# MLP weight sums moved from the up projection into the input projection; norms cut into three steps; output weights loaded one block ahead

## The chip, the cores and the metric

The kernel runs on one core of a Trainium2 chip. The metric is the device time of one execution in microseconds (us). Three executions of the kernel before took 2307.93, 2308.28 and 2311.22 us; the median is 2308.28 us.

## The reference

One layer of a streaming encoder, in float32, for 2048 prompt frames and 64 frames of a running stream (2112 tokens in all), model width 1024, MLP width 4096:

```
a = rmsnorm(h, norm1)
qa, ka, va, qr, kr, vr, gr = split(a @ w_in)          # width 2816: attention and retention heads
attn_o = windowed attention of qa, ka, va, with sinks
ret_o  = chunked retention of qr, kr, vr with decay; normed, times silu(gr)
h = h + concat(attn_o, ret_o) @ w_out
h = h + square(relu(rmsnorm(h, norm2) @ w_up)) @ w_down
y = rmsnorm(h, norm_f)
```

Outputs are y for both sets of frames, the newest 128 keys and values and the retention states.

## The kernel before, in words

Every float32 operand of a product is split into a high part h, written by ScalarE in the format fp32r, and a low part l = x - h, written by VectorE (`split`, L619: its lines are L620 and L621); each product is then three matmuls, hh, hl and lh. The kernel has four stages, one after the other.

**Input projection** (`group`, L516; main loop L570 to L587). Two phases `ph` of half the heads each; in each, 17 tiles `t` of 128 tokens (the last, `t = S = 16`, has 64); for each tile three groups `ci` of 384, 512 and 512 columns, 24 matmuls of 8 contraction blocks each (L529, L530, L532). Between the matmuls of a group, `run_ready` (L501) puts the attention and retention steps of earlier tiles (`att_b` to `att_e`, `ret_b` to `ret_e`). It is a planner with a clock of its own: `COST` (L478) is what a step takes of TensorE, `LAT` (L477) is how long after one step the next may be placed, doubled for the tiles in `slow` (L544). The pass runs under `manual_schedule` for TensorE and SyncE (L553): these two take their instructions in program order. VectorE, ScalarE and GpSimd take theirs in an order that the framework derives from a timing model when the kernel is built; the order is fixed then, and each engine runs it in order. VectorE does the rotations (L196 to L198), row maxima (L286), normalized weights (L301) and low parts here; GpSimd adds rotated parts (`zr` and `qk`, L199) and makes the low part of x (`xl`, L154). SyncE issues the loads: x of a tile (L142, one buffer `xr`), its rotation table (L160, two buffers `rt`). Weight loads go through the pool `wraw` (L74: four buffers of 4 KB a partition, tag `raw`): twelve loads at the start, twelve around the change of phase.

**Output projection** (`out_part`, L671). The 2112 tokens are three parts `p` of 704. For each of 8 output blocks `d` the weights of the block are loaded and split where they are used (L675 to L681, slots `wo`), the residual is loaded (`xres`, L683), 48 matmuls run (L690 to L692), the sum is stored to the scratch tensor `hscr` (L694), and ScalarE and GpSimd add up its squares (L696, L698). `load_mix` (L660) loads and splits the 8 mixed head blocks of a part. All of part 0 and part 1 is loaded before the first matmul (L747, L748), part 2 in a hook. `hooks` are steps put behind block `d`: the norm of the part before (`norm_part`, L704, through `norm_rs`, L623: a cast and a subtraction on VectorE, two matmuls with ones, then a scale, Sqrt on ScalarE, a reciprocal and four more steps on VectorE; twice per part, 352 columns each), and `a_sums` (L713: normed activations and their four right-hand sums, stored to `ascr`).

**Up projection** (`up_pair`, L798). Both MLP products are computed as 7 products of half-size blocks in place of 8 (the order is `ORDER`, L34). The right-hand sums come from `a_sums`. The left-hand (weight) sums are made by `left_sums` (L650): S5 = L21+L22 (L652, VectorE), S7 = L11-L21 (L653, GpSimd), S6 = S5-L11 (L654), S3 = L12-S6 (L655, both VectorE). A pass over the weights is 16 pairs `j` of 7 products of 12 matmuls, and there are three passes `p`. In pass 0, `up_weights` (L777) loads the two weight blocks of a pair, makes the sums, uses them and stores them to `uscr` (L785, L786). In passes 1 and 2 it loads the seven weights (L793), and behind each odd pair `down_sums` (L764) loads blocks of `wdn`, sums them and stores the sums to `sscr` (L774, L775). `norm_part(2)` stands behind pair 1 of pass 0 (L845); `a_operand` (L728) loads and splits the activations of the next pass behind the products of pair 15. The relu and square (L831, L832) and `right_sums` (L642) make the operands of the down projection, stored to `vscr` (L834, L835). From the output projection on, no engine is under `manual_schedule`.

**Down projection** (L948 to L1008). 84 steps of 48 matmuls (L970 to L972); it reads `wdn` or `sscr` (`left`, L863) and `vscr`, and ends with the last norm (`final_norm`, L896).

SBUF is close to full in both halves of the program. When the input projection ends (`p1.close()`, L592), the new pools lie where its pools lay, and the first writer of a new tile waits for the last reader of what lay there before (`reuse_waits="tile"`).

Of the kernel before, what the change touches and what calls it, by code (L numbers as in the profile page):

```python
# [11 lines left out]
F32 = mybir.dt.float32  # L12
# [19 lines left out]
NP = 3  # L32
# [7 lines left out]
def body(ctx, tc, xt, xtok, w1, wout, wup, wdn, gains, sinks, ck, cv, sret, rot, rdec, qdec, dmask,  # L40
# [528 lines left out]

    for i, (ph, t, ci) in enumerate(groups):  # L570
# [11 lines left out]
        group(ph, t, ci, n_)  # L582
        if (ph, ci) == (0, 2) and i == last_use[0, 2]:
            load_tables(1)
        if ph == 0 and i == last_use[0, ci]:
            ws[1, ci] = load_w(1, ci, raws)
            raws = None  # L587
    while queue:
        run_ready(1e9)
# [12 lines left out]
    wp = upper.enter_context(pool(name="wp", bufs=9, side="right"))  # L602
# [20 lines left out]
    def norm_rs(dst, acc, tmp):  # L623

        n = acc.shape[-1]
        pn_ = psum("pn_")
        ah, al = tmp("nah", F32R)[:, :n], tmp("nal", F32R)[:, :n]
        nc.vector.tensor_copy(ah, acc)
        sub(al, acc, ah.bitcast(F32))
        nc.tensor.matmul(pn_[:, :n], ones, ah, start=True, stop=False)  # L630
        nc.tensor.matmul(pn_[:, :n], ones, al, start=False, stop=True)
        m, y = tmp("nm", F32)[:, :n], tmp("ny", F32)[:, :n]
        nc.vector.tensor_scalar(m, pn_[:, :n], 1.0 / D, EPS, op0=ALU.mult, op1=ALU.add)
        nc.scalar.activation(y, m, AF.Sqrt)
        nc.vector.reciprocal(y, y)

        nc.vector.tensor_mul(m, m, y)
        nc.vector.tensor_mul(m, m, y)
        nc.vector.tensor_scalar(m, m, -0.5, 1.5, op0=ALU.mult, op1=ALU.add)
        nc.vector.tensor_mul(dst, y, m)  # L640
# [9 lines left out]
    def left_sums(sA, sB, L11, L12, L21, L22):  # L650

        add(sA[:, 0], L21, L22)  # L652
        nc.gpsimd.tensor_sub(sB[:, 0], L11, L21)  # L653
        sub(sA[:, 1], sA[:, 0], L11)  # L654
        sub(sB[:, 1], L12, sA[:, 1])  # L655

# [3 lines left out]
    def load_mix(p):  # L660
        n0 = p * PN
        out = []
        for f in range(8):
            raw = rawslot("mraw")[:, :PN]
            nc.sync.dma_start(raw, mscr[f, :, n0:n0 + PN])
            t = qp.tile([128, 2, PN], F32R, name="mhl", tag="q")
            split(t[:, 0], t[:, 1], raw)
            out.append(t)
        return out

    def out_part(p, mix, hooks):  # L671
        n0 = p * PN
        acc = None
        for d in range(NK):
            raw = rawslot("woraw")  # L675
            nc.sync.dma_start(raw, wout[d])
            w = []
            for i in range(2):
                s = wslot("wo")
                split(s[:, 0], s[:, 1], raw[:, i * 512:i * 512 + 512])  # L680
                w.append(s)  # L681
# [22 lines left out]
    def norm_part(p, acc):  # L704
        for b in range(2):
            tr, t = arslot("nr", F32R), arslot("nt")

            def tmp(name, dt):
                return (tr if dt == F32R else t)[:, int(name in ("nal", "ny"))]
            n = p * PN + b * NB  # L710
            norm_rs(rs2[:, n:n + NB], acc[:, b * NB:b * NB + NB], tmp)
# [23 lines left out]
    A, accs, mixes = {}, {}, {}  # L735
# [4 lines left out]
    def put(d, k, f, *a):  # L740
        d[k] = f(*a)

    with pool(name="op", bufs=1, side="right") as op:
        def opslot(name):
            return op.tile([128, 4, NB], F32, name=name, tag="as", bufs=2)
# [4 lines left out]
        accs[1] = out_part(1, mixes[1], {  # L750
            1: [lambda: norm_part(0, accs[0])],
            2: [later(a_sums, 0, 0, opslot), lambda: put(mixes, 2, load_mix, 2)],
            3: [later(a_sums, 0, 1, opslot)], 4: [later(a_sums, 0, 2, opslot)], 5: [later(a_sums, 0, 3, opslot)]})
        accs[2] = out_part(2, mixes[2], {
            1: [lambda: norm_part(1, accs[1]), lambda: put(A, (0, ORDER[0]), a_operand, 0, ORDER[0])],
            2: [lambda: put(A, (0, ORDER[1]), a_operand, 0, ORDER[1]), later(a_sums, 1, 0, opslot)],
            3: [lambda: put(A, (0, ORDER[2]), a_operand, 0, ORDER[2]), later(a_sums, 1, 1, opslot)],
            4: [lambda: put(A, (0, ORDER[3]), a_operand, 0, ORDER[3]), later(a_sums, 1, 2, opslot)],
            5: [later(a_sums, 1, 3, opslot)]})
        for i in ORDER[4:]:  # L760
            A[0, i] = a_operand(0, i)


    def down_sums(u):  # L764
        d, fq = u // 4, u % 4
        c = slice(fq * 512, fq * 512 + 512)
        rw = []
        for e in (d, d + 4):
            r = rawslot("dnraw").rearrange("p (a n) -> p a n", a=2)
            nc.sync.dma_start(r, wdn[e].rearrange("p (a f) n -> p a (f n)", a=2)[:, :, c])  # L770
            rw.append(r)
# [65 lines left out]
    with pool(name="up", bufs=1, side="right") as up:  # L837
        for p in range(NP):
# [114 lines left out]
    for n, (p, i, d) in enumerate(steps):  # L953
# [48 lines left out]
        for f in pending.pop(n, ()):  # L1002
            f()
# [97 lines left out]
```

## Time and profile before

| | |
|---|---|
| median of three executions | 2308.28 us |
| the profiled execution | 2315.14 us, its span 2313.3 us |
| TensorE busy | 2225.7 us (96%), mean granted clock 0.984 |
| VectorE busy | 1533.3 us (66%) |
| ScalarE busy | 1112.4 us (48%) |
| GpSimd busy | 474.2 us (20%) |
| DMA | 486.55 MB, mean 210 GB/s |

In the profile PE is TensorE's matmul, PEld its weight load, DVE VectorE, ACT ScalarE, POOL GpSimd, SP SyncE (SPq: its DMA issues). PEclk is the TensorE clock that the throttle granted, 1.00 being full speed. The view by stages gives for each stretch of the span the busy time and, in brackets, the instructions of each engine, then PEclk, the DMA share and the GB/s. The view of waits says which engine's line stood still for which other's, in us in total, how often, and the longest. The view of one line gives least, median and greatest duration in ns. The view in order of time gives start, duration, and in square brackets how long the engine was idle before and for whom it waited.

### The profile page before, as it was taken

What the parts mean: (1) busy time and instruction counts of PE and PEld (TensorE: products, weight loads), DVE (VectorE), ACT (ScalarE), POOL (GpSimd) and SP (SyncE); (2) the same over time, 40 slices, a digit from 0 to 9 for tenths busy, and PEclk for the clock granted to TensorE, in tenths of its full rate; (3) what the DMA queues carried; (4) which work ended last, traced back from release to release, by engine and by line L of the source; (5) the groups of instructions that cost most, each with busy time, mean ns of one, the idle gap of its engine ahead of it and who ended that gap; (6) DMA issues with size and microseconds to landing.
All of it is one profiled execution on the core that took longest, in us unless ns stands there. A gap on an engine that the chain in (4) does not pass through costs nothing.

```text
span 2313.3 us, 35596 instructions
## 1 busy us (share of the span) xinstructions
PE 2225.7 (96%) x13256; PEld 2117.4 (92%) x13256; DVE 1533.3 (66%) x2577; ACT 1112.4 (48%) x1985; POOL 474.2 (20%) x550
## 2 busy tenths in 40 slices
PE   7999999999997999699999999999999999999998
PEld 5888888888885999699999899999899999999998
DVE  5555556555556378887787768777766876687665
ACT  5444445443445243355555546655544544444452
POOL 5444343333332112110101000000000200020012
PEclk9999999999997999799999999999999999999999
DMA  6222233211115578866689999999986777677662
GB/s 191 79 69 69 76 95 118 61 43 52 48 33 191 177 269 290 287 233 233 232 291 355 344 321 335 335 318 303 354 286 235 253 275 259 223 270 283 237 212 78
DMA packets 242734, 486.55 MB, mean 210 GB/s; under 512 B 20560, under 2 KB 126224, under 8 KB 242560
## 3 DMA queue, kind: packets, MB, share of 16 engines
q1 hardware_dynamic: 238592, 474.40, 60.5%
q0 software_dynamic: 3968, 9.87, 1.4%
q8 instruction: 104, 1.70, 0.3%
q14 instruction: 70, 0.57, 0.1%
HBM read 348.28 MB, written 135.99 MB: 209 GB/s over the span
## 4 chain that ended last, share of the span: by engine, by line
PE 40%; DMA 9%; DVE 7%; issue 2%; ACT 1%; SPq 0%; DVEq 0%; POOL 0%; ACTq 0%
PE y L971 9%; PE y L972 9%; PE y L970 9%; DMA up<-in_wup 3%; DVE wu L621 2%; DMA upr<-uscr 2%; PE b L810 2%; PE b L811 2%; PE b L812 2%; PE a L812 1%; PE a L810 1%; PE a L811 1%; PE c L810 1%; PE c L811 1%; DMA sscr<-sd 1%
## 5 line engine op out<-in xcount | busy, mean ns | idle before, releaser
L971 PE MATMUL y<-vl,wd 128*128 128x352 f32 x1344 | 437.2, 325 | 0.0
L972 PE MATMUL y<-vh,wd 128*128 128x352 f32 x1344 | 435.0, 324 | 2.1 <-DVE wd L621 2.1
L970 PE MATMUL y<-vh,wd 128*128 128x352 f32 x1344 | 432.5, 322 | 0.3 <-ACT wd L620 0.3
L529 PE MATMUL z<-w,xh 128*128 128x512 f32 (+1 forms) x816 | 325.2, 398 | 7.1 <-ACT w L86 7.1
L530 PE MATMUL z<-w,xh 128*128 128x512 f32 (+1 forms) x816 | 309.2, 379 | 1.3 <-DVE w L87 1.3
L620 ACT ACTIVATE wd<-dr 128x1024 fp32r<-128x1024 f32 x168 | 177.3, 1057 | 254.9 <-PE y L972 176.3
L532 PE MATMUL z<-w,xl 128*128 128x512 f32 (+1 forms) x768 | 288.3, 375 | 0.5 <-POOL xl L154 0.3
L621 DVE TENSOR_TENSOR wd<-dr,wd 128x1024 fp32r<-128x1024 f32 x168 | 208.5, 1244 | 105.0 <-ACT wd L620 102.4
L972 PEld LDWEIGHTS y<-vh,wd 128*128 128x128 f32 x1344 | 252.3, 188 | 2.4 <-DVE wd L621 2.4
L970 PEld LDWEIGHTS y<-vh,wd 128*128 128x128 f32 x1344 | 253.8, 189 | 0.6 <-ACT wd L620 0.6
L971 PEld LDWEIGHTS y<-vl,wd 128*128 128x128 f32 x1344 | 251.9, 187 | 0.0
L810 PE MATMUL b<-ah,wu 128*128 128x352 f32 x576 | 187.4, 327 | 11.8 <-DVE u L821 9.4
L921 POOL TENSOR_TENSOR acc<-acc,sq 128x352 f32<-128x352 f32 x41 | 68.7, 1677 | 596.0 <-ACT sq L917 596.0
L812 PE MATMUL b<-ah,wu 128*128 128x352 f32 x576 | 186.4, 324 | 1.9 <-DVE wu L621 1.9
L811 PE MATMUL b<-al,wu 128*128 128x352 f32 x576 | 186.9, 324 | 0.0
L529 PEld LDWEIGHTS z<-w,xh 128*128 128x128 f32 x816 | 155.4, 190 | 26.0 <-ACT w L86 7.9
L620 ACT ACTIVATE wu<-upr 128x512 fp32r<-128x512 f32 x224 | 134.9, 626 | 89.8 <-DMA upr<-in_wup 50.7
L530 PEld LDWEIGHTS z<-w,xh 128*128 128x128 f32 x816 | 155.4, 190 | 22.9 <-DVE w L87 5.2
L621 DVE TENSOR_TENSOR wu<-upr,wu 128x512 fp32r<-128x512 f32 x224 | 149.7, 690 | 36.5 <-ACT wu L620 35.8
L532 PEld LDWEIGHTS z<-w,xl 128*128 128x128 f32 x768 | 144.2, 188 | 24.1 <-POOL xl L154 0.7
L621 DVE TENSOR_TENSOR vl<-rv,vh 128x1408 fp32r<-128x1408 f32 x84 | 137.2, 1638 | 37.9 <-ACT vh L620 36.4
L810 PE MATMUL a<-ah,wu 128*128 128x352 f32 x384 | 127.0, 331 | 15.2 <-ACT pc L815 8.0
(291 smaller groups left out, 4995.8 us busy)
## 6 DMA issues: line engine op xcount, KB each, us to landing
rv<-vscr SPq DMA_DIRECT2D x84, 704.0 KB, 5.5
vscr<-C SPq DMA_DIRECT2D x48, 1056.0 KB, 7.7
dr<-sscr SPq DMA_DIRECT2D x96, 512.0 KB, 4.3
dr<-in_wdn SPq DMA_DIRECT2D x72, 512.0 KB, 4.7
upr<-uscr SPq DMA_DIRECT2D x128, 256.0 KB, 6.5
upr<-in_wup SPq DMA_DIRECT2D x96, 256.0 KB, 6.4
up<-in_wup SPq DMA_DIRECT2D x32, 512.0 KB, 5.9
uscr<-su SPq DMA_DIRECT2D x32, 512.0 KB, 2.9
```

Source lines behind the costliest of these rows:

```text
L529: nc.tensor.matmul(z[:, :n], xh[:, k], wh, start=k == 0, stop=False)
L530: nc.tensor.matmul(z[:, :n], xh[:, k], wl, start=False, stop=k == NK - 1 and xl is None)
L532: nc.tensor.matmul(z[:, :n], xl[:, k], wh, start=False, stop=k == NK - 1)
L620: nc.scalar.activation(h, x, AF.Copy)
L621: sub(l, x, h.bitcast(F32))
L810: nc.tensor.matmul(o, wh, ah[:, k], start=k == 0 and i in (1, 6, 5), stop=False, skip_group_check=True)
L811: nc.tensor.matmul(o, wh, al[:, k], start=False, stop=False, skip_group_check=True)
L812: nc.tensor.matmul(o, wl, ah[:, k], start=False, stop=k == 3 and i in (2, 4, 3), skip_group_check=True)
L921: nc.gpsimd.tensor_add(self.acc, self.acc, sq)
L970: nc.tensor.matmul(o, wh, vh, start=f == 0, stop=False)
L971: nc.tensor.matmul(o, wh, vl, start=False, stop=False)
L972: nc.tensor.matmul(o, wl, vh, start=False, stop=f == 15)
```

## The change

- **Weight sums.** The sums of the up weights (32 units: block pair `j`, half `h`) and of the down weights (32 units: block `d`, one eighth of the columns) leave the up projection and are made during the input projection. A unit is 256 columns: two loads of 256 KB, four VectorE operations on 128x256, one store of 512 KB. Behind group i stand, in this order, the store of the unit that was loaded two groups earlier, the sums of the unit loaded one group earlier, and the loads of a new unit. The first unit is loaded behind group (phase 0, tile 2, 0); there are none in the groups about the change of phase nor in the first two tiles of phase 1. Loaded and summed tiles both come from `wraw`. All four sums are VectorE's; S7 was GpSimd's.
- **Up projection.** Pass 0 now reads its seven weights as the other two passes do. `down_sums` is gone. The small tiles `pc`, `u2`, `u3` are allocated together at the start of a pair.
- **Norms.** `norm_rs` becomes a class with three steps: `split`, `sums` (the matmuls with ones) and `power`. In the output projection and the first pairs of the up projection the steps of a part's norm stand behind three successive blocks or pairs, for all 704 columns at once; in the down projection behind three successive steps.
- **Output weights.** Those of block d+1 are loaded and split ahead of the matmuls of block d; those of block 0 ahead of everything else. `load_mix` loads one of 8 blocks per call; part 1's are loaded in hooks of part 0, part 2's in hooks of part 1.
- **Memory.** The pool `wp` of split weights has 8 buffers in place of 9.

```diff
+    def sum_load(u):
+        w, j, h = u // 32, u % 32 // 2, u % 2
+        r = wraw.tile([128, 4, 256], F32, name="sr", tag="raw")
+        if w == 0:
+            c = slice(h * 256, h * 256 + 256)
+            src = [wup[e].rearrange("p (a c) -> p a c", a=2)[:, :, c] for e in (j, j + 16)]
+            dst = uscr[:, j, :, c]
+        else:
...
+        for k in range(2):
+            nc.sync.dma_start(r[:, 2 * k:2 * k + 2], src[k])
+        return r, dst
+    def sum_make(r, dst):
+        s = wraw.tile([128, 4, 256], F32, name="st", tag="raw")
+        L11, L12, L21, L22 = (r[:, k] for k in range(4))
+        nc.vector.tensor_add(s[:, 0], L21, L22)
+        nc.vector.tensor_sub(s[:, 2], L11, L21)
+        nc.vector.tensor_sub(s[:, 1], s[:, 0], L11)
+        nc.vector.tensor_sub(s[:, 3], L12, s[:, 1])
+        return s, dst
+    def sum_store(s, dst):
+        nc.sync.dma_start(dst.rearrange("s p c -> p s c"), s)
...
         group(ph, t, ci, n_)
+        if made:
+            sum_store(*made.pop())
+        if loaded:
+            made.append(sum_make(*loaded.pop()))
+        if todo and (first <= i < change or ph == 1 and t > 1):
+            loaded.append(sum_load(todo.pop(0)))
...
-    wp = upper.enter_context(pool(name="wp", bufs=9, side="right"))
+    wp = upper.enter_context(pool(name="wp", bufs=8, side="right"))
...
+            w = wnext.pop()
+            if (p, d) != (NP - 1, NK - 1):
+                wnext.append(load_wout((d + 1) % NK))
...
-        mixes[0] = load_mix(0)
-        mixes[1] = load_mix(1)
-        accs[0] = out_part(0, mixes[0], {})
+        wnext.append(load_wout(0))
+        for f in range(8):
+            load_mix(0, f)
+        accs[0] = out_part(0, {d: [later(load_mix, 1, 2 * (d - 2) + k) for k in range(2)] for d in range(2, 6)})
...
-                if (p, j) == (0, 1):
-                    norm_part(2, accs[2])
+                if p == 0 and j == 0:
+                    n2 = norm_part(2, arslot)
+                if p == 0 and 1 <= j <= 3:
+                    n2[j - 1]()
                 if p == 1 and j in (2, 4, 6, 8):
                     a_sums(2, j // 2 - 1, arslot)
-                if p > 0 and j % 2:
-                    down_sums(8 * (p - 1) + j // 2)
```

More of the change, by code (lines that the diff above doesn't have):

```diff
@@ L587, in body @@
             raws = None
+    assert not todo and not loaded and not made
     while queue:
@@ L648, in body, with load_mix, load_wout, out_part @@
     RIGHT = {1: 0, 2: 1, 3: 2, 5: 3, 7: 4, 6: 5, 4: 6}
[L650 to L655, printed above, removed]
-    LEFT = {5: 0, 6: 1, 7: 2, 3: 3}
-    def load_mix(p):
-        n0 = p * PN
-        out = []
[L663 to L668, printed above, removed]
+    LEFT = {5: 0, 6: 1, 7: 2, 3: 3}
+    def load_mix(p, f):
+        raw = rawslot("mraw")[:, :PN]
+        nc.sync.dma_start(raw, mscr[f, :, p * PN:p * PN + PN])
+        t = qp.tile([128, 2, PN], F32R, name="mhl", tag="q")
+        split(t[:, 0], t[:, 1], raw)
+        mixes.setdefault(p, []).append(t)
+    def load_wout(d):
+        raw = rawslot("woraw")
+        nc.sync.dma_start(raw, wout[d])
+        out = []
+        for i in range(2):
+            s = wslot("wo")
+            split(s[:, 0], s[:, 1], raw[:, i * 512:i * 512 + 512])
+            out.append(s)
         return out
-    def out_part(p, mix, hooks):
+    def out_part(p, hooks):
         n0 = p * PN
@@ L674, in out_part @@
         for d in range(NK):
[L675 to L681, printed above, removed]
+            w = wnext.pop()
+            if (p, d) != (NP - 1, NK - 1):
+                wnext.append(load_wout((d + 1) % NK))
+            mix = mixes[p]
             xres = op.tile([128, PN], F32, name="xres", bufs=3)
```

154 lines of the change are left out of this document (76 added, 78 removed).

## The prediction

> **What bounds the kernel now.** I read the page first, then the view by stages, then the waits of each stage that loses time.
>
> ```profile
> span 2313.3 us, 35596 instructions
> ...
> PE 2225.7 (96%) x13256; PEld 2117.4 (92%) x13256; DVE 1533.3 (66%) x2577; ACT 1112.4 (48%) x1985; POOL 474.2 (20%) x550
> ...
> PE   7999999999997999699999999999999999999998
> ...
> PEclk9999999999997999799999999999999999999999
> ```
>
> TensorE is the bound over the whole span. The two dents, in slices 13 and 17, are idle time, and the clock dips with them. The change takes away no matmul, so all it can win is time in which TensorE stands still or runs slowly. The view by stages gives their size.
>
> ```profile
> 100.00:717.00 617.00, 616.40 (x3502) 541.42 (x3501) 340.06 (x884) 275.86 (x841) 241.52 (x358) 1.00 0.24 69
> 717.00:750.00 33.00, 15.87 (x72) 10.64 (x70) 21.80 (x44) 20.75 (x49) 9.16 (x15) 0.63 0.73 258
> 750.00:937.00 187.00, 187.00 (x1161) 187.00 (x1162) 125.44 (x178) 63.12 (x93) 38.24 (x21) 0.99 0.74 252
> 937.00:1173.00 236.00, 209.54 (x1241) 204.01 (x1241) 185.75 (x293) 116.86 (x170) 30.70 (x16) 0.95 0.70 239
> 1173.00:1409.00 236.00, 226.11 (x1371) 222.45 (x1370) 179.93 (x295) 132.10 (x187) 15.70 (x8) 0.99 0.98 330
> 1409.00:1646.00 237.00, 230.92 (x1429) 229.00 (x1428) 176.10 (x284) 135.78 (x190) 14.02 (x8) 1.00 0.96 322
> 1646.00:2300.00 654.00, 651.77 (x4045) 651.49 (x4045) 445.28 (x465) 314.17 (x321) 68.75 (x41) 1.00 0.70 248
> ...
> 1350.00:1400.00 50.00, 50.00 (x313) 50.00 (x312) 37.37 (x65) 28.71 (x45) 2.59 (x2) 1.00 0.94 320
> ```
>
> The rows are the input projection, the passage to the output projection, the output projection, the up projection in three equal stretches (near enough its passes) and the down projection. The last row is an undisturbed stretch of the up projection: 50.00/313 = 0.1597 us a matmul. At that pace the three stretches need 1241, 1371 and 1429 times 0.1597, that is 198.2, 219.0 and 228.2 us; they took 236, 236 and 237. So they lose 37.8, 17.0 and 8.8 us, 63.6 together. The passage loses 17.1 us idle (33.00 - 15.87) and, at a clock of 0.63, some 5.9 more (15.87 x 0.37): 23. The other stages lose next to nothing. These 87 us are the prize.
>
> **Up projection: what leaves it.** The waits of the up projection:
>
> ```profile
> PE b L810 <- DVE u L821: 9.4, 10, 3.2
> PE a L810 <- ACT pc L815: 8.0, 1, 8.0
> PE pn__10243 L630 <- DVE nr L628: 6.9, 1, 6.9
> PE a L810 <- ACT wu L620: 6.3, 3, 2.6
> PE pn__10243 L631 <- DVE nr L629: 2.4, 1, 2.4
> PE b L810 <- DVE u L818: 2.3, 4, 0.7
> PE c L810 <- DVE C L822: 2.3, 5, 0.6
> ```
>
> Nearly all of it is VectorE running late, with one great lump at the norm: 6.9 + 2.4 + 8.0 = 17.3 us of TensorE idle. What makes VectorE late is in the next rows.
>
> ```profile
> DVE su L652 <- DMA up<-in_wup: 26.1, 9, 4.5
> ...
> L655 DVE TENSOR_TENSOR su<-up,su x16: 679/1614/2193, 892.4 to 1160.4; 128x512 f32<-128x512 f32 x16
> ...
> L653 POOL TENSOR_TENSOR su<-up,up x16: 1274/1577/4505, 892.4 to 1160.5; 128x512 f32<-128x512 f32 x16
> ```
>
> In pass 0 the sums stand at the head of VectorE's queue while their weights are still on the way (26.1 us in 9 waits), with the low parts and the reads of PSUM behind them. L655, a 0.68 us subtraction, took a median of 1.61 beside GpSimd's L653. All this goes: the wait, three operations a pair, and the GpSimd operation. In passes 1 and 2 `down_sums` goes, with 16 units in each of four VectorE or GpSimd operations, 1 MB in and 1 MB out. DMA at 330 and 322 GB/s was near full there (share 0.98, 0.96); 16 x 2.1 MB less is 34 MB over two passes of 236 us, 71 GB/s less, so the 6.3 us of late weight splits (L620) goes too. Pass 0 now loads 7 x 262 KB a pair where it loaded 1.05 MB and stored 1.05: 0.26 MB less.
>
> What is late next: VectorE still has the splits and the `right_sums`, ScalarE the relu and square, and pass 1 keeps `a_sums`. The third stretch, where sums stood behind only every second pair, lost 8.8 us, part of it at the change to the down projection. I leave 14 us for the whole stage, a little under half of that rate in each stretch with a surplus for the first pairs; the bounds are 4 (nothing but the passage to the next stage) and 26 (8.8 in each). Gain 50, bounds 38 and 60.
>
> The norm in three steps is inside this number. A reservation: L630 first ran at 952.4, right behind pair 0, though the code has it behind pair 1. The order follows what the timing model takes for ready, so the three places are a wish.
>
> ```profile
> 952.41 0.32 PE L630 MATMUL pn__10229<-nr,ones 128*128 128x352 f32 x1
> ```
>
> With VectorE on time, the 17.3 us go all the same; if it should be late again at the norm, that is their price.
>
> **The passage.**
>
> ```profile
> PE y L690 <- ACT wo L620: 6.3, 1, 6.3
> ...
> 749.18 3.24 ACT L620 ACTIVATE wo<-woraw 128x512 fp32r<-128x512 f32 x6 [5.18 <-DMA mscr<-mix]
> ...
> L621 DVE TENSOR_TENSOR mhl<-mraw,mhl 128x704 fp32r<-128x704 f32 x24 | 21.1, 931 | 1.0 <-ACT mhl L620 1.0
> ```
>
> The first weights of the output projection are split only when the very last store of the attention tail has landed: the new tile lies on the memory of `mix`. From the sizes in the code, the right side held 61,024 bytes a partition before `p1` closed; `wr` and nine `wp` buffers take 61,440, so the last buffer reaches into the neighbour pool, where `mix` lies. Eight take 57,344 and do not. Then weights and mixed blocks can be split as soon as the last projection matmul is done (717), and only 8 blocks, not 16, stand ahead of the first matmul. If TensorE takes matmuls of the output projection between the steps of the tail, as it took L630 early, most of the 23 us goes; if it keeps the tail first, the 6.3. I take 14: the 23 less 8 mixed blocks at 0.93 us each (L621), rounded; bounds 4 and 23. Inside the output projection the stage is full (187.00 of 187.00); loads of blocks moved into hooks and weights split one block ahead I cost at 0: VectorE is busy 125 of 187 us, covering them; if that cover failed, each late block would show as a wait on `mhl` or `wo`. The norm of the last stage, now three steps behind each other, costs 0 too: TensorE idles 2.2 us in 654, and nothing waits for y.
>
> **The input projection: what is added.** 64 units of four VectorE operations on 128x256. The nearest rows, both reading two SBUF tensors:
>
> ```profile
> L233 DVE TENSOR_TENSOR hl<-zr,hl 128x384 fp32r<-128x384 f32 x29 | 16.2, 557 | 8.4 <-ACT hl L231 7.8
> ...
> L432 DVE TENSOR_TENSOR hl<-cf,hl 128x64 fp32r<-128x64 f32 x1 | 0.2, 220 | 0.0
> ```
>
> Between them 256 columns come to 220 + 337 x 192/320 = 422 ns, so 1.7 us a unit, 108 us in all. One tile from the middle shows where they fit.
>
> ```profile
> 505.21 0.87 POOL L199 TENSOR_TENSOR zr<-rot,rot 128x320 f32<-128x320 f32 x1 [2.86 <-DVE rot L198]
> ...
> 512.82 1.28 POOL L199 TENSOR_TENSOR qk<-rot,rot 128x512 f32<-128x512 f32 x1 [4.29 <-DVE rot L198]
> ...
> 518.68 2.39 POOL L154 TENSOR_TENSOR xl<-xr,xh 128x1024 fp32r<-128x1024 f32 x1 [4.21 <-DVE sd L376]
> ...
> 526.22 0.87 POOL L199 TENSOR_TENSOR zr<-rot,rot 128x320 f32<-128x320 f32 x1 [2.50 <-DVE rot L198]
> ```
>
> A tile takes 526.22 - 505.21 = 21.0 us, a group 7.0, so the units spread over 448 us. VectorE goes from 340.06/617 = 55% to 55 + 24 = 79% there. DMA goes from 69 GB/s to 69 + 67 MB/448 us = 219, under the 330 that the up projection had.
>
> ```profile
> 510.86 0.75 DVE L196 SCALAR_TENSOR_TENSOR rot<-z,rs,rt 128x512 f32<-128x512 f32 x1 [3.52 <-PE z L532]
> ...
> 516.47 1.01 DVE L301 TENSOR_SCALAR p<-p,sm 128x192 f32<-128x192 f32 x4
> ```
>
> ```profile
> 515.05 0.60 PE L362 MATMUL ptr<-idf,qk 128*128 128x128 f32 x4
> ...
> 519.06 1.04 PE L312 MATMUL pt<-idf,p 128*128 128x128 f32 x8
> ```
>
> VectorE had one gap of 3.52 us in this tile alone, room for eight operations. Two spares decide: from L301's end (517.48) to L312 1.58 us, from the end of `qk` (514.10) to L362 0.95. One sum in front of a critical operation costs 0.42, inside both. A wait of a sum for its loads holds all of VectorE's queue (rotations, maxima, L301) and behind it TensorE. The nearest row of a scheduled load into a computing engine in this stage:
>
> ```profile
> ACT xk L164 <- DMA xk<-in_xtok: 10.9, 15, 1.2
> ...
> SPq L160 <- DVE rot L198: 310.7, 28, 14.1
> ```
>
> 10.9/15 = 0.73 us late, inside the spares. SyncE stands 310.7/28 = 11 us a time waiting for a rotation buffer, so the three DMAs of a unit find room; its stores wait for the sums, and behind them stand x (L142) and rotation loads, which it issues about a tile (21 us) ahead. GpSimd gets no instruction, only neighbours. I take 6 us: a tenth of a microsecond a unit, near the 0 of the spares; bounds 0 and 34 (next part).
>
> A rule speaks against this term. The row first: L655 took 1.61 where it takes 0.68 alone, beside a GpSimd operation that reads SBUF. The Trainium skill, SBUF — State Buffer, section "Who interferes with whom", says that a VectorE instruction with two SBUF inputs contends with a GpSimd instruction that reads SBUF, and that whoever starts first holds the shared port to the end. By it a sum that begins under `xl` would hold VectorE for up to GpSimd's whole operation; the sum of this prediction would then go by the second rival.
>
> **The sum.** Gains 50 + 14, cost 6: 58 us off. Against the profiled execution 2315.14 - 58 = 2257; that execution lies 6.9 us above the median, so on the median's scale 2308.3 - 58 = 2250.
>
> **The rivals.** *The up stage keeps its own waits.* The second and third stretch lost 25.8 us with VectorE at 76% and 74%, and the splits alone may do that. Then only the first falls, to 8.8: gain 29 + 14 - 6 = 37, 2271. Against it: the 50 us quoted above ran without a gap.
>
> *VectorE and GpSimd hold each other up.* If each `xl` catches a sum, L301 can be late by 2.39 + 0.42 - 1.58 = 1.2 us; `qk`, at 1.28 + 0.42 - 0.95 = 0.75 every second tile, adds 0.4. That is 1.6 us in 64/3 = 21 tiles: 34 us, so 64 - 34 = 30 gained, 2278. For it: L655. Against it: `xl` runs where TensorE has just been served. By the skill's port rule this is what happens wherever the two meet.
>
> *Slower: the sums wait for late loads.* In the up projection a wait on L652 was 26.1/9 = 2.9 us. If each of 64 units waited so in the input projection, TensorE would lose 2.9 - 1.58 = 1.3 us by the wider spare and 2.0 by the narrower: 84 to 125 us, so 2328 to 2369. It decides from 1.0 us lost a unit (64 us against gains of 64). Against it are the 0.73 us above and two groups between load and sums.
>
> *The norm isn't spread*, since the order is the timing model's: 17.3 us stay, 2268.
>
> **How the numbers follow.** Forecast 0.58 (its own range 2232 to 2266), own waits 0.12, port 0.14, norm 0.06, slower 0.07, and 0.03 for a balance near zero. The range 2228 to 2292 takes in the upper bound of each gain (60 + 23 - 3 gives 2228) and the middle rivals with some surplus. A measurement of this kernel tells about 0.2%, 4.6 us, from no change: faster 0.90, same 0.03, slower 0.07.
>
> **What would show it.** Right: the three passes of the up projection each near 219 us at a DMA share under 0.9, no wait above 3 us at the norm, the first output matmul under 743 on a scale where the projection ends at 717 plus its new losses, and TensorE over 99% in the input projection. Wrong: waits of L312, L362 or L373 repeating once a tile; `xl` or the sums' longest duration over 3 us with such waits; VectorE waiting for `sr` loads by more than 1 us; or L821 and L818 still holding L810 for 10 us and more.

## The result, and the profile after

The kernel got slower: 2349.7 us (median of 4 runs, 2344.2 to 2351.8) against 2308.2 us for the kernel before on the same chip (2307.9 to 2311.2), a ratio of 1.0173 with a 95% interval of 1.0153 to 1.0193. The forecast was 2250, the range 2228 to 2292. What happened is the rival on the other side, to which the prediction gave 0.07. The profiled execution took 2350.85 us and has a span of 2349.1 us, 35.8 more than before.

From the page after: its span, the busy time, and the rows of TensorE and its clock over 40 slices.

```profile
span 2349.1 us, 35902 instructions
...
PE 2241.0 (95%) x13256; PEld 2128.2 (91%) x13256; DVE 1575.1 (67%) x2716; ACT 1113.4 (47%) x1982; POOL 425.0 (18%) x518
...
PE   7998889988889999989999999999999999999998
```

The dents of before, in slices 13 and 17, are gone or smaller. In their place slices 4 to 6 and 9 to 12 stand at 8: a thin loss over the whole input projection, which hardly shows at this resolution; the 8 of slice 18 is the start of the up projection. The first and last start of the matmuls of each stage give its size. These are rows of the views of the tiles `z`, `y` and `a` of the kernel after (instruction, count, shortest/median/longest ns, first and last start).

```profile
L529 PE MATMUL z<-w,xh x816: 331/396/793, 7.4 to 809.3; 128*128 128x512 f32 x109, 128*128 128x384 f32 x55
L530 PE MATMUL z<-w,xh x816: 332/394/688, 8.0 to 809.6; 128*128 128x512 f32 x109, 128*128 128x384 f32 x55
...
L735 PE MATMUL y<-mhl,wo x384: 317/322/622, 825.2 to 1017.4; 128*128 128x352 f32 x192
...
L840 PE MATMUL a<-ah,wu x384: 320/322/495, 1017.9 to 1673.6; 128*128 128x352 f32 x192
...
L1003 PE MATMUL y<-vh,wd x1344: 320/324/661, 1680.7 to 2335.3; 128*128 128x352 f32 x192
```

The input projection is 809.6 - 7.4 = 802.2 us, the passage 825.2 - 809.6 = 15.6, the output projection 1017.9 - 825.2 = 192.7 and the up projection 1680.7 - 1017.9 = 662.8. The same rows in the other kernels give this table; its last columns are the median of the whole and the ratio to the kernel before, which ran beside the experiments at medians of 2311.6 to 2312.5. The stages are those of one profiled execution of each kernel, worked out before rounding; whole executions of one kernel differ by 2 to 13 us, so small differences between rows are not to be leaned on.

| kernel | input | passage | output | up | median us | ratio to before, 95% interval |
|---|---|---|---|---|---|---|
| before | 710.0 | 32.7 | 187.1 | 709.1 | 2308.2 | 1 |
| after | 802.2 | 15.6 | 192.7 | 662.8 | 2349.7 | 1.0153 to 1.0193 |
| e1_no_sums | 710.5 | 15.6 | 192.4 | 662.8 | 2259.5 | 0.9764 to 0.9797 |
| e2_pinned | 733.6 | 15.6 | 191.2 | 664.2 | 2281.6 | 0.9853 to 0.9883 |
| e3_not_moved | 710.7 | 15.6 | 192.6 | 699.3 | 2289.4 | 0.9887 to 0.9921 |
| e4_moved_only | 806.4 | 32.9 | 187.2 | 673.0 | 2374.1 | 1.0254 to 1.0285 |
| e5_far | 821.7 | 15.6 | 192.1 | 662.4 | 2368.1 | 1.0217 to 1.0262 |
| e6_resident | 747.8 | 15.6 | 191.6 | 662.4 | 2294.2 | 0.9902 to 0.9944 |
| e7_pin_gaps | 757.0 | 14.3 | 193.4 | 672.2 | 2319.0 | 1.0013 to 1.0043 |
| e8_pin_gaps2 | 787.8 | 15.4 | 197.1 | 672.8 | 2350.6 | 1.0145 to 1.0190 |
| e9_free | 731.3 | 15.7 | 191.9 | 665.6 | 2280.4 | 0.9846 to 0.9879 |
| e10_pin_maxima | 750.1 | 15.6 | 192.1 | 663.9 | 2299.4 | 0.9934 to 0.9970 |

The down projection is 657.7 to 659.7 in all of them. The change won 46 us in the up projection and 17 in the passage, gave back 5.5 in the output projection, and lost 92 in the input projection. The view by stages of the kernel after says the same of TensorE's busy time (columns as in the prediction).

```profile
100.00:809.00 709.00, 649.08 (x3529) 559.70 (x3528) 448.34 (x1131) 278.89 (x852) 250.07 (x366) 0.97 0.54 151
...
1017.00:1233.00 216.00, 206.15 (x1263) 204.76 (x1262) 158.29 (x252) 119.05 (x171) 5.93 (x2) 0.98 0.75 250
1233.00:1449.00 216.00, 216.00 (x1352) 216.00 (x1351) 164.18 (x268) 130.08 (x185) 0.00 (x0) 1.00 0.85 292
```

The middle third of the up projection is now full, 216.00 of 216.00. The input projection was full before; now TensorE stands idle for 709.00 - 649.08 = 59.9 us of the first row, and its granted clock has come down to 0.97. Who waits there stands in the waits of the kernel after between 60 and 810 us (total, times, longest).

```profile
DVE st L590 <- DMA sr<-in_wdn: 57.9, 24, 4.0
...
DVE st L590 <- DMA sr<-in_wup: 38.5, 20, 3.3
PE pq L247 <- DVE hl L233: 36.4, 17, 4.9
...
PE pr L383 <- DVE sd L376: 8.0, 6, 1.9
```

L590 is the first of a unit's four VectorE operations. In 44 of the 64 units VectorE stands before it until the load has landed, 96.4 us in all, 2.2 us a time. Behind it in VectorE's queue stand the low parts of the attention's queries and keys (L233) and the scores of the retention (L376), and for these TensorE waits. One such place, from VectorE's and SyncE's timelines of the kernel after (start, duration, engine, operation; in brackets the idle time before it and its releaser):

```profile
505.72 0.42 DVE L217 CAST kw<-pk 128x256 fp32r<-128x256 f32 x1 [0.37 <-ACT kw L215]
509.52 1.20 DVE L590 TENSOR_TENSOR st<-sr 128x256 f32<-128x256 f32 x1 [3.38 <-DMA sr<-in_wdn]
...
511.32 0.54 DVE L286 TENSOR_REDUCE mx<-s 128x2 f32<-128x384 f32 x1
```

```profile
502.58 1.52 SPq L583 DMA_DIRECT2D sr<-in_wdn  x2
```

SyncE issued both halves of the load at 502.6 to 504.1. VectorE finished L217 at 506.1, came to L590 next, and stood 3.38 us. The row maxima L286, which need no weights, started at 511.3. In the code this unit's sums stand behind the last rotation of the next group, L198. On VectorE that rotation comes 13.6 us after them, as a later row of the same timeline shows:

```profile
523.08 0.47 DVE L198 SCALAR_TENSOR_TENSOR rot<-z,rs,rt 128x256 f32<-128x256 f32 x1
```

It is so in all 64 units: the sums start 13 to 33 us ahead of the operation that the code puts in front of them (L198, L233 or L356 by turns). How close they stand to their loads shows in the first and last start of both, from the view of the tile `sr`:

```profile
L583 SPq DMA_DIRECT2D sr<-in_wup x64: 539/598/1760, 68.7 to 324.3; - x64
L590 DVE TENSOR_TENSOR st<-sr x64: 410/425/3312, 75.0 to 702.4; 128x256 f32<-128x256 f32 x64
...
L583 SPq DMA_DIRECT2D sr<-in_wdn x64: 544/611/1534, 330.7 to 698.0; - x64
```

The first sum starts 6.3 us behind its load, the last 4.4; over all units it is 4.4 to 9.8, with a median of 6.5. Where VectorE waits, this is the load's own time, and VectorE had come to the sum before. A group of matmuls is 7.0 us. The code puts one whole group between a load and its sums; in VectorE's queue that distance does not exist. That queue's order is not the order of the code: only TensorE and SyncE run in the order in which the code was written there, and VectorE's instructions are put in order when the kernel is built, by a model of the times.

### The profile page after: what moved, and what is told of

The parts are those of the page before. It is cut to its first block, busy times and chain, and to the rows that moved or that the text cites. A ratio compares the mean times of both kernels' runs of the same rounds, so it can differ in the third digit from the quotient of the medians.

```text
span 2349.1 us, 35902 instructions
## 1 busy us (share of the span) xinstructions
PE 2241.0 (95%) x13256; PEld 2128.2 (91%) x13256; DVE 1575.1 (67%) x2716; ACT 1113.4 (47%) x1982; POOL 425.0 (18%) x518
## 4 chain that ended last, share of the span: by engine, by line
PE 71%; DMA 11%; DVE 9%; issue 4%; SPq 2%; POOL 2%; ACT 1%; DVEq 0%; POOLq 0%; ACTq 0%
PE y L1004 9%; PE y L1005 9%; PE y L1003 9%; DMA sr<-in_wup 5%; PE b L840 4%; PE b L841 4%; PE b L842 4%; DMA sr<-in_wdn 3%; PE z L529 3%; PE z L530 3%; PE c L841 3%; PE c L842 3%; PE c L840 3%; PE a L842 2%; PE a L841 2%
## 5 line engine op out<-in xcount | busy, mean ns | idle before, releaser
L529 PE MATMUL z<-w,xh 128*128 128x512 f32 (+1 forms) x816 | 331.0, 406 | 7.4 <-ACT w L86 7.4
L530 PE MATMUL z<-w,xh 128*128 128x512 f32 (+1 forms) x816 | 315.3, 386 | 1.0 <-DVE w L87 1.0
L532 PE MATMUL z<-w,xl 128*128 128x512 f32 (+1 forms) x768 | 293.9, 383 | 0.0
L659 ACT ACTIVATE wu<-upr 128x512 fp32r<-128x512 f32 x336 | 209.3, 627 | 162.3 <-PE b L842 92.3
L660 DVE TENSOR_TENSOR wu<-upr,wu 128x512 fp32r<-128x512 f32 x336 | 230.6, 691 | 73.6 <-ACT wu L659 56.9
L529 PEld LDWEIGHTS z<-w,xh 128*128 128x128 f32 x816 | 159.1, 195 | 26.2 <-ACT w L86 7.4
L530 PEld LDWEIGHTS z<-w,xh 128*128 128x128 f32 x816 | 159.0, 195 | 22.7 <-DVE w L87 4.4
L532 PEld LDWEIGHTS z<-w,xl 128*128 128x128 f32 x768 | 148.1, 193 | 24.1
L659 ACT ACTIVATE vh<-rv 128x1408 fp32r<-128x1408 f32 x84 | 116.0, 1381 | 52.2 <-DMA rv<-vscr 31.7
```

Of the source, the lines that this page charges most:

```text
L529: nc.tensor.matmul(z[:, :n], xh[:, k], wh, start=k == 0, stop=False)
L530: nc.tensor.matmul(z[:, :n], xh[:, k], wl, start=False, stop=k == NK - 1 and xl is None)
L532: nc.tensor.matmul(z[:, :n], xl[:, k], wh, start=False, stop=k == NK - 1)
L659: nc.scalar.activation(h, x, AF.Copy)
L660: sub(l, x, h.bitcast(F32))
```

## The experiments

Theory A: VectorE's order has each sum where the model expects its load to have landed; the load lands some 2 us later, VectorE's queue stands, and TensorE with it. Theory B: the cost is VectorE's 108 us of added work itself, with the time that its operations and GpSimd's hold each other up. Theory C: the loads and stores in SyncE's queue and on the DMA engines delay x and the rotations.

**Four kernels that take the change apart.** e1_no_sums leaves out the four VectorE operations; the loads stay, and the loaded tile itself is stored.

```
-        nc.vector.tensor_add(s[:, 0], L21, L22)
...
-        return s, dst
+        return r, dst
```

> The changed kernel with the four VectorE operations of a unit left out: the loaded tile itself is stored, so the sums are not computed (uscr and sscr hold unsummed blocks). Loads, stores and their places in SyncE's queue stay. The input projection (first to last projection matmul) took 710 us before and 802 after. Theory A, VectorE's queue stands behind sums whose loads have not landed: it falls to 710 to 720 and the kernel to about 2262 us. Theory B, the sums' own work and the port that they share with GpSimd hold VectorE up: the same, since both go. Theory C, the added DMA traffic and SyncE's longer queue make x late: it stays over 780 us, the kernel over 2325.

It took 2259.5 us, with 710.5 us for the input projection. Its view by stages and its waits of TensorE between 60 and 735 us:

```profile
100.00:717.00 617.00, 614.94 (x3488) 539.13 (x3487) 338.56 (x881) 274.80 (x839) 240.36 (x356) 1.00 0.60 170
```

```profile
PE pss L373 <- ACT rkT L367: 4.0, 2, 3.8
PE pr L383 <- ACT vs L349: 1.8, 4, 0.9
PE prt L417 <- DVE ro L409: 1.6, 1, 1.6
```

The DMA engines move 170 GB/s here, against 69 before, with 192 DMAs more in SyncE's queue, and TensorE does not feel it. Theory C falls for the kernel after: there too ScalarE waits for x only 1.3 us in the whole stage. (In e1_no_sums no store has to wait for sums; kernels in which many do come below.) It also shows what the change is worth without that work: a ratio of 0.9781.

e2_pinned is the whole computation. A unit's four operations may not be placed ahead of the last VectorE operation of the group behind which the code has them: the low part L233, the rotation L198 or the gate L356.

```
+        pin[0] = nc.vector.tensor_sub(hv[:, :, 1], zr[:T], hv[:, :, 0].bitcast(F32))
...
-            made.append(sum_make(*loaded.pop()))
+            with tc.issue_after(pin[0].ins):
+                made.append(sum_make(*loaded.pop()))
```

> The changed kernel, complete, with one thing more: in VectorE's order the sums of a unit may not stand ahead of the last VectorE operation of the group behind which the code has them (hl, the last rotation or the gate). Work, loads and stores are the same. Theory A (sums placed where the timing model takes the loads for landed, a few us too early): the waits on sr fall from 96 us to under 30, the input projection from 802 to 715 to 740 us, the kernel to 2262 to 2287. Theory B (work and port): the input projection stays over 780, the kernel over 2325. Theory C (traffic, SyncE): likewise over 780.

It took 2281.6 us, ratio 0.9868, 1.3% faster than before. The tile `sr` of this kernel (the engine's idle time before it stands in the last row):

```profile
L583 SPq DMA_DIRECT2D sr<-in_wup x64: 544/712/1356, 69.2 to 306.1; - x64
L590 DVE TENSOR_TENSOR st<-sr x64: 412/418/1107, 88.7 to 658.3; 128x256 f32<-128x256 f32 x64
...
L583 SPq DMA_DIRECT2D sr<-in_wdn x64: 544/612/1951, 311.8 to 645.9; - x64
...
  DMA sr<-in_wdn: 0.7, 1
```

The same loads, at the same places of SyncE's queue; the sums now stand 88.7 - 69.2 = 19.5 us behind the first load and 12.4 behind the last, and in all units 0.3 to 1.1 us behind the start of the operation that the code puts in front of them. VectorE waits 0.7 us for them instead of 96.4, and the input projection is 68.6 us shorter. Theory A has most of the loss; 23.1 us above e1_no_sums remain.

e3_not_moved keeps the sums in the up projection as before (`up_weights(p, j)` and `down_sums` with it), with the other parts of the change; e4_moved_only is the kernel before with the sums moved alone, so with its one-piece norm, nine buffers and late output weights. The core of each, the first against the kernel after, the second against before:

```
-            loaded.append(sum_load(todo.pop(0)))
...
+                if p > 0 and j % 2:
+                    down_sums(8 * (p - 1) + j // 2)
```

```
+            loaded.append(sum_load(todo.pop(0)))
...
-                if p > 0 and j % 2:
-                    down_sums(8 * (p - 1) + j // 2)
```

> The changed norms, output weights, order of loads and 8 buffers, but the weight sums stay in the up projection as in the kernel before. It measures what those parts are worth by themselves. If the passage and the norm each pay as the changed kernel's trace suggests (passage 33 to 16 us, less 5 lost in the output projection, norm waits 17 us): 2308 - 12 - 17 = about 2280. If the norm lumps come from the sums and not from the norm's form: about 2296, with over 8 us of waits at the norm left.

> Only the weight sums moved; norms, output weights and buffers as before. If the input projection's loss comes from the sums alone, it takes 795 to 810 us again; the up projection keeps the norm's waits of up to 17 us of the 46 us that it gained, and the passage its 33 us: the kernel at 2365 to 2380. If the up projection's gain is the sums' alone, it takes 663 to 668 us here too and the kernel 2355 to 2365.

They took 2289.4 and 2374.1 us: the first between its two cases, the second as expected. In the up projection the moved sums alone gave 709.1 - 673.0 = 36.1 us, the rest alone 709.1 - 699.3 = 9.8; together 45.9, and the whole change gave 46.3. In the passage it is the other way round: 32.9 with the moved sums alone, 15.6 with the rest. The parts add up, and the loss of the input projection belongs to the sums: 806.4 with them alone, 710.7 without.

**Is it the distance in the code?** e5_far makes the sums in place, so that all four buffers take loads, and puts them three groups behind the load in the code.

```
+        nc.vector.tensor_add(L22, L21, L22)
...
-        if loaded:
-            made.append(sum_make(*loaded.pop()))
+        if loaded and loaded[0][0] + 3 <= i:
+            made.append(sum_make(*loaded.pop(0)[1]))
```

> As the kernel after, but the sums are made in place in the loaded tile, which leaves all four buffers to loads, and a unit's sums stand three groups behind its load in the code where they stood one group behind; nothing pins them. Theory A (the order on VectorE is fixed at build time, by when a model of the times takes the load to have landed, so the distance in the code decides nothing, only the lead that the model sees): the waits for sr stay, 50 us or more, the input projection stays at 770 us or more, the time at 2317 to 2355. Rival, too little lead in the code: with two more groups, 14 us, each load has landed, no wait for sr is left, the input projection falls to that of the pinned kernel, 734 or less, the time to 2282 or less.

2368.1 us, slower still. The waits and the stage are as theory A had them; the time lies above its 2317 to 2355. The tile `sr` of this kernel, and VectorE's waits between 60 and 740 us:

```profile
L583 SPq DMA_DIRECT2D sr<-in_wup x64: 544/600/709, 69.0 to 337.9; - x64
L589 DVE TENSOR_TENSOR sr<-sr x64: 410/426/1552, 74.7 to 740.8; 128x256 f32<-128x256 f32 x64
...
L583 SPq DMA_DIRECT2D sr<-in_wdn x64: 544/603/1476, 456.3 to 736.3; - x64
```

```profile
DVE sr L589 <- DMA sr<-in_wdn: 74.8, 29, 4.5
DVE sr L589 <- DMA sr<-in_wup: 57.3, 27, 4.7
```

With three groups, 21 us, in the code the first sum starts 5.7 us behind its load and the last 4.5, as with one group; all sums start 28 to 48 us ahead of the operation that the code puts in front of them. The distance in the code decides nothing; the rival of too little lead falls. That the loads are later here, since each waits in SyncE's queue for its buffer's store (239.0 us in 56 waits), may be what makes it slower than the kernel after; that was not tried by itself.

**What do the operations cost without a wait?** e6_resident let them read two tables that lie in SBUF.

```
-        L11, L12, L21, L22 = (r[:, k] for k in range(4))
-        nc.vector.tensor_add(s[:, 0], L21, L22)
+        x, y = (tabs[ph][k].rearrange("p a b -> p (a b)") for k in range(2))
+        nc.vector.tensor_add(s[:, 0], x, y)
```

> As the kernel after, with all loads, all stores and four VectorE operations a unit in the same form, unpinned; but the operations read two tables that lie in SBUF, so what they store is not the sums of the weights and the loaded tile is not read. Theory A (the wait for the loads is the cost): without it the input projection comes to 712 to 736 us, the time to 2260 to 2284. Theory B (the cost is VectorE's own 108 us of work, with the time that its operations and GpSimd's hold each other up): it stays at 780 or more, the time at 2327 or more. Between them the 92 us are shared out by what is left.

747.8 us lies between the theories, and the waits tell why: between 60 and 740 us, 51.1 us in 21 waits of L590 for `sr` were left. A unit's output tile takes a buffer that a load still fills. The experiment did not take away what it was to take away. e9_free gives the output a scratch tile of its own:

```
+    wsum = p1.enter_context(tc.tile_pool(name="wsum", bufs=1))
...
+        s = wsum.tile([128, 4, 256], F32, name="sx", tag="sx")
...
+        return r, dst
```

> The clean form of e6_resident, in which a unit's output tile still took a buffer that waited for a load. All loads stay, and each loaded tile is stored as it is, as in e1_no_sums; the four VectorE operations a unit read two tables that lie in SBUF and write into a scratch tile of their own that nobody reads, unpinned, so the sums are left out and only their work stays (three loading buffers, not four, to make room). If the wait for the loads is all that VectorE adds to the 92 us: input projection 711 to 718. If the 23 us that the pinned kernel still loses are the price of VectorE's work, wherever it stands: 728 to 740, the time 2276 to 2290. If the work and the port shared with GpSimd are the main cost: 760 or more, 2308 or more.

2280.4 us, the input projection 731.3. The operations never wait for a weight load, and 731.3 - 710.5 = 20.8 us are the price of VectorE's work. So two ways of ending the waits, pins and resident operands, end within 2.3 us of each other. Two reservations. TensorE waits some 3 us longer than in e1_no_sums for its first weights (9.9 + 1.5 against 7.7 + 0.7), probably because three buffers load them instead of four. And with nothing to wait for, the sums run earlier, from 38.5 to 492.1 us where the kernel after has them from 75.0 to 702.4, so they stand beside other work. Rows of its tile `sx`:

```profile
L591 DVE TENSOR_TENSOR sx<-qd,dm x64: 404/424/2476, 38.5 to 487.3; 128x256 f32<-128x256 f32 x64
...
L594 DVE TENSOR_TENSOR sx<-dm,sx x64: 390/418/3765, 43.6 to 492.1; 128x256 f32<-128x256 f32 x64
```

But e2_pinned, whose sums run from 88.7 to 658.3, pays 23.1, nearly the same, if through other waits of TensorE. Part of what this price is shows in two rows of the timelines of e2_pinned, VectorE's and GpSimd's:

```profile
507.26 0.41 DVE L590 TENSOR_TENSOR st<-sr 128x256 f32<-128x256 f32 x1
507.59 1.50 DVE L591 TENSOR_TENSOR st<-sr 128x256 f32<-128x256 f32 x1
```

```profile
507.43 1.39 POOL L199 TENSOR_TENSOR qk<-rot,rot 128x512 f32<-128x512 f32 x1 [2.65 <-DVE rot L198]
```

L591 has the form of L590 and takes 1.50 us where L590 takes 0.41: it starts while GpSimd's rotation runs, until 508.82, and ends at 509.09. By the rule that the prediction took from the Trainium skill, SBUF — State Buffer, section "Who interferes with whom", the operation that comes second waits for the port; this trace agrees. Whether this, or simply the longer queue, makes the 21 us was not separated.

**Better places for the pins?** e7_pin_gaps and e8_pin_gaps2 make the sums in place and move the pins: `behind` is called with L233, L409 and, in the first, L356, in the second L316. They also issue the loads of `a_sums` one block earlier. e10_pin_maxima calls it with L233, L356 and the row maxima L287, and leaves `a_sums` alone.

```
+    def behind(ins):
+        if loaded and loaded[0][0] < now[0]:
+            with tc.issue_after(ins.ins):
+                made.append(sum_make(*loaded.pop(0)[1]))
...
+            hooks[3 + k].append(later(a_early, 0, k, opslot))
+            hooks[4 + k].insert(0, later(a_late, 0, k))
```

> The whole computation. Sums in place; a tile's three units are pinned on VectorE behind the low part L233, behind the gate's last operation L356 and behind the retention's last product L409 (the kernel e2_pinned had the third behind the rotation of the second group, in front of the row maxima). Also, the load of the blocks for the right sums of the output projection is issued one block of eight matmul groups ahead, and those sums are pinned behind that block's residual addition. If the 23 us that e2_pinned still lost come from where its units stood: input projection 712 to 726 us, and the 7.5 us wait at the start of the up projection gone, 2259 to 2275 in all. If they are the price of VectorE's work itself, wherever it stands: input projection 730 to 736, 2272 to 2278 by the right sums alone.

> The whole computation. As e7_pin_gaps, with the unit that it pins behind the gate's operation pinned behind the low part of the attention's weights, L316, instead, the last VectorE operation before the second product of the attention. If the place decides: within 712 to 730 us for the input projection, and a difference from e7_pin_gaps of several us either way. If VectorE's work itself is the price: 730 to 736 as there, and no difference.

> The whole computation. As e2_pinned, with sums in place, the store of a unit a full group behind its sums as there, and the unit that stood behind the rotation of the second group, in front of the row maxima, now pinned behind those maxima (L287). If the place of that unit makes the late transposed keys (6.4 us in 17 waits of TensorE in e2_pinned): input projection 715 to 728, the time 2263 to 2277. If e7_pin_gaps lost its time by its stores, which stood in SyncE's queue ahead of the sums, this one comes out within 5 us of e2_pinned, 729 to 739; if it lost it by where its units stood, 745 or more.

757.0, 787.8 and 750.1 us, all worse than e2_pinned. e7_pin_gaps misses both its cases. e8_pin_gaps2 misses its ranges too, but the difference from e7_pin_gaps that its first case asked for is there, 30.8 us. e10_pin_maxima falls into its last case, 745 or more, which was to mean that the places cost and not the stores; its trace says otherwise. VectorE does not wait for a load at all there, and the late transposed keys fell from 6.4 us in 17 waits to 2.0 in one. In their place stand these rows of its waits between 60 and 735 us:

```profile
PE pr L391 <- ACT vs L357: 24.5, 15, 3.0
...
ACT xh L160 <- DMA xr<-in_xt: 66.7, 18, 5.6
```

ScalarE waits for x (`xr`), which it hardly did in the kernel after (1.3 us), and 14 of TensorE's 15 waits, 24.1 us, come right behind such a wait. One of them, from the timelines of VectorE, SyncE, ScalarE and TensorE:

```profile
225.01 0.42 DVE L600 TENSOR_TENSOR sr<-sr 128x256 f32<-128x256 f32 x1
```

```profile
225.46 0.37 SPq L604 DMA_DIRECT2D uscr<-sr  x1
225.93 3.00 SPq L591 DMA_DIRECT2D sr<-in_wup  x4
228.98 0.61 SPq L149 DMA_DIRECT2D xr<-in_xt  x1
```

```profile
234.96 1.06 ACT L160 ACTIVATE xh<-xr 128x1024 fp32r<-128x1024 f32 x1 [3.72 <-DMA xr<-in_xt]
```

```profile
236.32 0.49 PE L391 MATMUL pr<-vs,sd 128*128 128x128 f32 x2 [1.12 <-ACT vs L357]
```

The store L604 stands in SyncE's queue until the last sum L600 is done; behind it stand two units' loads, and behind them the load of x. Such a store is the last thing that SyncE waited for ahead of 10 of the 18 late loads of x. In e7_pin_gaps it is so for 19 of 23: ScalarE waits 64.4 us for x, and the 21.9 us that TensorE waits there for `hl` and `kw` of ScalarE come shortly behind such waits. So by the traces theory C, which fell for the kernel after, is at work in these kernels: sums that run late hold their stores, and the stores hold x. e2_pinned has late x too (46.1 us in 21 waits of ScalarE), but of its 17 late transposed keys only one stands behind such a wait. e7_pin_gaps and e8_pin_gaps2 also still wait for weight loads, 16.3 and 27.8 us. How much of their loss is x, and how much the places on VectorE, was not separated; no run tried the stores on another queue. e2_pinned, the first try, stays the best of the whole computations. The earlier loads for `a_sums` made the up projection longer by some 8 us than in e2_pinned: the wait of 7.5 us at its start went, and one of 14.7 for `u` came.

## Why the prediction was wrong

**The up projection: right in size.** 46.3 us of a forecast 50, inside 38 to 60. The second third became full and the last nearly (229.08 of 231.00); the first still idles 9.9 us, 7.3 of them in one wait that is shown below. The late weight splits fell from 6.3 us to 0.7, and VectorE's waits for `up` went. The norm's 17.3 us went too, but not by the ground that the prediction gave, that they go once VectorE is on time. With the sums moved and the norm as it was they are all there. TensorE's waits of e4_moved_only after 1030 us:

```profile
PE a L825 <- ACT pc L830: 9.4, 1, 9.4
PE pn__10817 L668 <- DVE nr L666: 5.5, 1, 5.5
PE pn__10817 L669 <- DVE nr L667: 2.4, 1, 2.4
```

That is 9.4 + 5.5 + 2.4 = 17.3 us again. In e3_not_moved, with the sums in place and the norm in three steps, no wait at the norm is longer than 1.2 us. So the form of the norm ends them; here the number was right by luck.

**The passage: near.** 17.1 us of a forecast 14 (its working, 23 less eight times 0.93, gives 15.6 and not 14), but the output projection, costed at 0, gave 5.5 back: passage and output projection together fell from 219.8 to 208.3, 11.5 us. The waits on `wo` at the start are gone; the last attention steps now run between output matmuls, so part of the passage has only moved into the next stage.

**The input projection: the step that failed.** It was costed at 6 us and lost 92.2. Two statements carried the 6. The first was the nearest row for a scheduled load, ScalarE's `xk`, 0.73 us late: a size, and too small, since a sum waited 2.2 us in 44 of 64 units. The row that the prediction set aside for its slow rival, 2.9 us on L652, was much nearer. The second failed outright: "two groups between load and sums". That distance stood in the code; on VectorE the sums ran 13 to 33 us ahead of their place in the code and came to most of the loads before these had landed (each half lands 3.3 to 7.0 us after its issue, by the view of L583). The prediction had written of the norm that "the order follows what the timing model takes for ready, so the three places are a wish", and did not hold that sentence against the sums, which lie on the same engine and in the same order. With it, the rival at 84 to 125 us deserved more than 0.07. The two spares that were to decide were also not the ones that ran out: TensorE waited 3.8 us at L312 and 2.7 at L362, but 36.4 at L247 for the low parts L233, in 17 waits, where in the kernel before it did not once.

The 92.2 us come apart so: 0.5 for the DMAs (e1_no_sums), 20.8 for VectorE's work without waits (e9_free), 2.3 more in the pinned kernel, 68.6 that went with the pins. The 0.5 may be scatter, since e3_not_moved, which has none of these DMAs, took 0.7 more than before; the 2.3 is likewise a difference of two single executions. The last term holds the waits, from 96.4 us on VectorE to 0.7, and with them whatever the pins' places changed; the other pinned kernels warn that the two can't be told apart to the microsecond.

**The rivals.** The slower one happened as described: waits of the sums, VectorE's queue, then TensorE. That 92.2 us fall into its 84 to 125 is in part luck: it had all 64 units wait 2.9 us where 44 wait 2.2, and it did not count VectorE's work; the waits alone come to some 68.6/64 = 1.07 us a unit, just over its point of decision at 1.0. The port rival (34 us) is not the main cause, but the 21 us are of its order. The up stage did not keep its own waits, and the norm was spread: its matmuls start at 1068.3, 50 us into the stage. SyncE's queue cost nothing in the kernel after, as forecast, but it did in the kernels with other pins. In the range, the 3 us that are taken from 60 + 23 come from no row.

What is argued and not shown: that the model counts the landings too early. The runs show that VectorE's order has the sums far ahead of their place in the code, whether that is one group behind the load or three, that in 44 of 64 units it comes to them before the load has landed, and that pinning the order ends the waits.

The same thing still stands in e2_pinned and in the kernel after at the start of the up projection. From VectorE's timeline and TensorE's waits of the kernel after:

```profile
1025.52 1.81 DVE L766 SCALAR_TENSOR_TENSOR ra<-ra,gsb,rs 128x704 f32<-128x704 f32 x2 [4.51 <-DMA ra<-hscr]
```

```profile
PE a L842 <- DVE wu L660: 7.3, 1, 7.3
```

VectorE comes to the scaling of `a_sums` before its load has landed, and the low parts of the first weights of the up projection stand behind it.

## What to carry to other kernels

A distance between a load and its use counts on the engine that uses it, not in the code: where the order on that engine is made at build time, read in a trace when the load is issued and when the engine comes to its user, or pin the user behind an operation that runs late enough. Work that waits for DMAs is dear at the head of a queue that feeds the bottleneck, even if that engine is only 55% busy; price its wait by the nearest row on the same engine. And when such work is moved later, look at what stands behind its stores in the queue that issues them: here it was x, and other pins, which looked as free in the timeline, lost 16 to 54 us of the input projection against the first.

## What was not expected of the hardware

Traffic of 170 GB/s beside a full TensorE, where it was 69 before, cost nothing that can be told from scatter: 710.5 us against 710.0 for the input projection (e1_no_sums). A VectorE operation of 128x256 with two inputs in SBUF took 1.50 us beside a GpSimd operation and 0.41 without; the prediction's 0.42 was right for the bare operation. And where TensorE's idle time came in short pieces, its granted clock came down as well: 0.97 over the input projection with 59.9 us idle, 1.00 in e1_no_sums with 2.06.
